# Opening chunks of two tiles by four heads, one token-major load, and later stages in an encoder trunk

## The chip, the cores and the metric

The kernel runs on one core of a Trainium2 chip. The metric is the device time of one execution in microseconds (us). Three runs of the kernel before gave 2071.57, 2072.32 and 2072.38 us, median 2072.32. Beside them one execution was recorded by the hardware profiler.

The core has TensorE (PE in the profile; its weight loads are PEld), VectorE (DVE), ScalarE (ACT), GpSimd (POOL) and SyncE (SP), which here only issues DMAs. Each takes its instructions in a fixed order and waits on semaphores.

## The reference

A trunk of two layers on 256 tokens of width 2048, all in float32. Layer 0 mixes tokens by grouped-query attention (16 query heads, 4 key and value heads of width 128, RMS norm on queries and keys, axial rotary positions), layer 1 by a gated linear recurrence in two directions. A SwiGLU feed-forward of inner width 5632 follows each.

```python
def attention_mixer(h, w_qkv, q_gain, k_gain, w_o, cos, sin):
    qkv = h @ w_qkv
    q, k, v = jnp.split(qkv, [N_Q_HEADS * HEAD_DIM, (N_Q_HEADS + N_KV_HEADS) * HEAD_DIM], axis=-1)
    ...
    q = apply_axial_rope(rms_norm(q, q_gain), cos, sin) * (HEAD_DIM ** -0.5)
    k = apply_axial_rope(rms_norm(k, k_gain), cos, sin)
    ...
    return o @ w_o

def swiglu(h, w_gate, w_up, w_down):
    return (jax.nn.silu(h @ w_gate) * (h @ w_up)) @ w_down

def reference(x, ...):
    for i in range(DEPTH):
        h = rms_norm(x, norm_mix[i])
        ...
        x = x + mix
        x = x + swiglu(rms_norm(x, norm_ffn[i]), ffn_w_gate[i], ffn_w_up[i], ffn_w_down[i])
    return x
```

## The kernel before, in words

The activations lie transposed: 16 tiles x_sb[k] of 128 features by 256 tokens. Every large product runs over k tiles of 128 features. To keep float32 accuracy on a faster number format, each weight and each activation is split into a high part (rounded) and a low part (the rest): ScalarE casts the raw weights to the high part (line 93), VectorE subtracts it for the low part (line 94). For one k tile TensorE multiplies the high part of the weights with both parts of the activation (512 columns) and the low part with the high part of the activation (256 columns), both into one PSUM accumulator "acc" (line 165). Such a pair is called a block here. step() counts blocks, and later(delay, fn) puts small pieces of TensorE work behind a fixed number of them, one at a time; TensorE's order is thus written out by hand. The order on the other engines and on the DMA queue of SP is made by a scheduler when the kernel is built.

Weights come in chunks of eight tiles of 128 by 128 (512 KB), in the order of the list "order". half() takes the next one: load_half loads it into a "raw" tile, casts and subtracts. raw, hi and lo have five buffers each, so chunks are cast up to five ahead of TensorE.

The stages of layer 0, as far as the change touches them:

- Opening. All four key heads are accumulated at once in the four accumulators. A key chunk holds four k tiles of two heads. The first chunk is loaded and split in three pieces (2, 2 and 4 tiles) with x in between; load_x loads x tiles and scales them by the norm's gain at once (ScalarE line 252, VectorE line 255, tile "xg"). Ten idle matmuls (line 229) stand ahead of it.
- The norm's mean square per token is folded in later: token_squares loads x token-major in four chunks, each into a raw tile, in between the last key and the first value chunks, and squares it on ScalarE (line 335). first_rms, FIRST = 17 blocks after the keys, makes the sums and spreads them by a small matmul (line 359).
- Keys. key(h) evacuates the accumulator (ScalarE copy line 208, VectorE add line 209), rotates, squares (line 381); KEYS blocks later a matmul sums the squares (line 388), and the key is scaled and split into kT[h]. Values are transposed 21 blocks after their product and split into vt[h].
- Queries. attend(h): evacuation, rotation on POOL (on VectorE for the last head), split into qs (lines 213, 214). Then, after delays that USUAL or LATE give: sums (transposes and squares), scores (six matmuls, the maxima on VectorE at lines 447 and 448, Exp on ScalarE, POOL scales the probabilities at line 457), turn (four transposes, copies to pT), values (six matmuls). The delays of turn and values count from the stage before.
- Output. output() runs the first half of k for four columns (FRONT), then k tiles 8 to 13 of two more chunks that it holds, then flush() runs all stages that still wait, and only then do k tiles 14 and 15 follow. The same function ends the recurrence of layer 1, whose last act tiles are made at line 651 and split at lines 213 and 214. Afterwards the norm's sums are spread by a matmul (line 274), NORM = 9 blocks later.
- Feed-forward. Units (gate and up columns) in three parts of 16, 14 and 14, each followed by its down product over 16 columns. Between parts one unit of the next part is computed ahead of the down product; the last part has none.

## Time and profile before

| what | value |
|---|---|
| median of three runs | 2072.32 us |
| the profiled execution's own time | 2072.61 us |
| its span on the core | 2070.8 us |
| granted TensorE clock, mean over the span | 0.999 |
| ScalarE, share of the span busy | 52% |
| POOL, share of the span busy | 19% |
| DMA, mean over the span | 187 GB/s |
| read from HBM | 382.13 MB |

The rows quoted further on come from the page of this execution and from answers of its trace. A row of a timeline starts with the start and the length in us, then engine, line, operation, out<-in, shape and count; in brackets stands the idle time of the engine just before it and what ended it. A row of waits reads: who waited for whom, us in total, times, longest. A row that groups instructions gives busy us and the mean ns of one, then the idle time before them. A row of windows gives the stretch, its length, then busy us and count of PE, PEld, DVE, ACT and POOL (or of PE alone), the granted TensorE clock, the busy share of the DMA engines and GB/s. Line numbers are those of the kernel before.

### The profile page before, as it was taken

The numbers are of one execution on the slowest core, as the hardware profiler recorded it, in microseconds if no ns is written. First come the engines' busy times: TensorE is split into PE (matmuls) and PEld (weight loads), VectorE is DVE, ScalarE is ACT, GpSimd is POOL, SyncE is SP. The second block draws the span as 40 slices with busy tenths as digits, with TensorE's granted clock in tenths as the row PEclk, the third lists the DMA queues.
The fourth block names the chain that finished last, engine by engine and source line by source line (L and its number), as shares of the span: only waits on it lengthen the run. The fifth ranks groups of instructions, "written<-read, shape, count | busy, mean of one in ns | idle before, by whom it ended". The sixth has DMA issues, their size and how long they took to land.

```text
span 2070.8 us, 32880 instructions
## 1 busy us (share of the span) xinstructions
PE 2060.8 (100%) x12528; PEld 1829.3 (88%) x12528; DVE 1448.1 (70%) x2152; ACT 1069.3 (52%) x1603; POOL 389.0 (19%) x394
## 2 busy tenths in 40 slices
PE   9999999999999999999999999999999999999999
PEld 7898888888888888888999998888888888888888
DVE  7889876665666666668878878766665666666665
ACT  7666444443344434444589995544443444444442
POOL 1463521110011000113334433311100111001100
PEclk9999999999999999999999999999999999999999
DMA  8544655555555565556655545555555555565564
GB/s 296 166 138 148 218 184 186 191 191 186 192 186 191 176 192 201 184 183 187 195 178 178 190 153 193 182 191 190 192 186 190 188 189 184 183 202 186 192 191 136
DMA packets 112766, 386.39 MB, mean 187 GB/s; under 512 B 12640, under 2 KB 15072, under 8 KB 112608
## 3 DMA queue, kind: packets, MB, share of 16 engines
q1 hardware_dynamic: 112464, 384.26, 56.5%
q8 instruction: 99, 1.62, 0.3%
q14 instruction: 59, 0.48, 0.1%
q10 hardware_dynamic: 144, 0.02, 0.0%
HBM read 382.13 MB, written 2.10 MB: 186 GB/s over the span
## 4 chain that ended last, share of the span: by engine, by line
PE 91%; POOL 4%; DVE 3%; issue 1%; ACT 1%; DMA 0%; SPq 0%; POOLq 0%; ACTq 0%; DVEq 0%
PE acc L165 80%; PE acc L175 3%; PE acc L176 3%; PE acc L177 3%; POOL hb L374 2%; DVE lo L94 1%; PE pm L176 1%; PE pm L177 1%; PE pm L175 1%; POOL pr L457 1%; POOL hq L375 1%; POOL hq L376 1%; ACT L309 0%; DMA raw<-in_w_k_dram 0%; ACT sg L309 0%
## 5 line engine op out<-in xcount | busy, mean ns | idle before, releaser
L94 DVE TENSOR_TENSOR lo<-raw,hi 128x1024 fp32r<-128x1024 f32 (+1 forms) x722 | 886.4, 1228 | 352.9 <-ACT hi L93 343.5
L93 ACT CAST hi<-raw 128x1024 fp32r<-128x1024 f32 (+1 forms) x722 | 741.7, 1028 | 594.6 <-PE acc L165 409.7
L165 PE MATMUL acc<-xg,hi 128*128 128x512 f32 x3200 | 1013.3, 396 | 1.8 <-DVE xg L255 1.7
L165 PEld LDWEIGHTS acc<-xg,lo 128*128 128x128 f32 x3200 | 601.4, 188 | 142.0 <-DVE lo L94 3.1
L165 PE MATMUL acc<-xg,lo 128*128 128x256 f32 x3200 | 638.4, 279 | 1.0 <-DVE lo L94 0.9
L165 PE MATMUL acc<-act,hi 128*128 128x512 f32 x1892 | 596.5, 396 | 0.1
L165 PEld LDWEIGHTS acc<-xg,hi 128*128 128x128 f32 x3200 | 490.7, 189 | 2.9 <-DVE xg L255 2.2
L165 PEld LDWEIGHTS acc<-act,lo 128*128 128x128 f32 x1892 | 355.4, 188 | 84.8 <-DVE act L213 1.3
L165 PE MATMUL acc<-act,lo 128*128 128x256 f32 x1892 | 372.9, 278 | 1.0 <-DVE act L213 1.0
L525 POOL TENSOR_TENSOR fg<-fg,nr 128x256 f32<-128x256 f32 x88 | 118.7, 1349 | 1187.3 <-ACT fg L309 1187.3
L165 PEld LDWEIGHTS acc<-act,hi 128*128 128x128 f32 x1892 | 288.9, 189 | 0.3 <-DVE act L214 0.3
L175 PE MATMUL acc<-xg,hi 128*128 128x256 f32 x512 | 144.8, 283 | 0.0
L176 PE MATMUL acc<-xg,hi 128*128 128x256 f32 x512 | 144.6, 282 | 0.0
L177 PE MATMUL acc<-xg,lo 128*128 128x256 f32 x512 | 144.4, 282 | 0.0
L208 ACT COPY fg<-acc 128x256 f32<-128x256 f32 x88 | 33.0, 375 | 152.9 <-PE acc L165 152.9
L208 ACT COPY fu<-acc 128x256 f32<-128x256 f32 x88 | 32.9, 374 | 148.2 <-PE acc L165 148.2
L177 PEld LDWEIGHTS acc<-xg,lo 128*128 128x128 f32 x512 | 97.9, 191 | 0.0
L175 PEld LDWEIGHTS acc<-xg,hi 128*128 128x128 f32 x512 | 97.9, 191 | 0.0
L176 PEld LDWEIGHTS acc<-xg,hi 128*128 128x128 f32 x512 | 97.9, 191 | 0.0
L209 DVE TENSOR_TENSOR fg<-acc,fg 128x256 f32<-128x256 f32 x88 | 37.4, 425 | 79.7 <-ACT fg L208 79.6
L209 DVE TENSOR_TENSOR fu<-acc,fu 128x256 f32<-128x256 f32 x88 | 37.4, 425 | 74.3 <-ACT fu L208 74.3
L291 DVE TENSOR_TENSOR x<-x,acc 128x256 f32<-128x256 f32 x126 | 52.9, 420 | 41.8 <-PE acc L165 41.8
(171 smaller groups left out, 1435.5 us busy)
## 6 DMA issues: line engine op xcount, KB each, us to landing
raw<-in_w_gate_dram SPq DMA_DIRECT2D x176, 512.0 KB, 3.6
raw<-in_w_up_dram SPq DMA_DIRECT2D x176, 512.0 KB, 3.6
raw<-in_w_down_dram SPq DMA_DIRECT2D x128, 512.0 KB, 3.6
raw<-in_w_in_dram SPq DMA_DIRECT2D x64, 512.0 KB, 3.9
raw<-in_w_down_dram SPq DMA_DIRECT2D x64, 384.0 KB, 3.1
raw<-in_w_qv_dram SPq DMA_DIRECT2D x40, 512.0 KB, 3.8
raw<-in_w_o_dram SPq DMA_DIRECT2D x32, 512.0 KB, 3.7
raw<-in_w_out_dram SPq DMA_DIRECT2D x32, 512.0 KB, 3.7
```

Of the source, the lines that this page charges most:

```text
L93: act.copy(hi[:, sl, :], raw[:, sl, :])
L94: dve.tensor_tensor(lo[:, sl, :], raw[:, sl, :], hi[:, sl, :].bitcast(F32), ALU.subtract)
L165: pe.matmul(o, w, x, start=(k == 0 and not part), stop=(k == total - 1 and not part))
L175: pe.matmul(o, hi, x[:, :S], start=start, stop=False)
L176: pe.matmul(o, hi, x[:, S:], start=False, stop=False)
L177: pe.matmul(o, lo, x[:, :S], start=False, stop=stop)
L208: act.copy(t, acc[:, S:])
L209: dve.tensor_tensor(t, acc[:, :S], t, ALU.add)
L291: dve.tensor_tensor(x_sb[j], x_sb[j], acc[:, :S], ALU.add)
L374: eng.tensor_tensor(b[64 * j : 64 * j + 64], y[64 * i : 64 * i + 64], s[64 * i : 64 * i + 64], ALU.mult)
L375: eng.tensor_tensor(dst, y, c, ALU.mult)
L525: pool.tensor_tensor(g, g, norm.r, ALU.mult)
```

## The change

- The key chunks are cut otherwise: the first six hold two k tiles of all four heads, the last two four k tiles of two heads (KEY_TILES). The first chunk is loaded whole and split in four pieces, the second in two. x tiles are loaded as before, but scaled in pairs, one pair ahead of each chunk's cast, and held in ScalarE's order behind the newest cast (follow).
- The token-major x becomes one 2 MB load into a tile of its own (x_tok), placed on SP behind the first two value chunks, which are taken ahead of the keys' evacuation. When its squares are done, the same place ("kv") holds kT and vt. Its squares run in two pairs, one after the evacuation of keys 0 and 1, one after the cast of the fourth value chunk.
- FIRST goes from 17 to 22, KEYS to (29, 31, 35, 41); the first head has its own delays (FIRST_HEAD), and the last three heads have new ones (LATE).
- The split of a query into qs is issued 8 blocks after its product (OPERAND) and held on VectorE behind the newest maxima, those of the head before.
- output() holds three chunks instead of two (HELD), so 18 blocks instead of 12 stand ahead of flush(); the norm behind it is finished 11 blocks later instead of 9.
- In the last part of a feed-forward, the first two columns of the down product are begun together: first half of k for both, then second half of both.

```diff
 FRONT = 4
+HELD = 3
-FIRST = 17
+FIRST = 22
 NORM = 9
-KEYS = (24, 26, 30, 33)
+KEYS = (29, 31, 35, 41)
 VALUE = 21
+FIRST_HEAD = (17, 22, 16, 10)
 USUAL = (17, 22, 15, 7)
-LATE = ((10, 23, 15, 13), (5, 15, 17, 9))
+LATE = ((17, 22, 15, 12), (10, 23, 15, 13), (7, 16, 16, 9))
+OPERAND = 8
...
+KEY_TILES = [[(2 * i + k, j) for j in range(NKV) for k in range(2)] for i in range(KT // 2 - 2)]
+KEY_TILES += [[(KT - 4 + k, j + h) for h in range(2) for k in range(4)] for j in (0, 2)]
...
+    def follow(i, j):
+        tc.add_manual_dep(i.ins, j.ins.name, ...)
+        return i
...
-    def load_half(src, n, pieces=None):
+    def load_half(src, n, pieces=1, then=None):
...
+        newest["load"] = sync.dma_start(out=raw[:, :n, :], in_=src[:, :n, :])
+        if then:
+            then()
+        for i in range(pieces):
+            sl = slice(i * n // pieces, (i + 1) * n // pieces)
+            newest["cast"] = act.copy(hi[:, sl, :], raw[:, sl, :])
             dve.tensor_tensor(lo[:, sl, :], raw[:, sl, :], hi[:, sl, :].bitcast(F32), ALU.subtract)
...
-            seq += more[:1] + [halves(w[f"w_down{l}_{p}"][j], n) for j in range(KT)] + more[1:]
+            down = [halves(w[f"w_down{l}_{p}"][j], n) for j in range(KT)]
+            if not more:
+                down[:2] = [down[j][i : i + 1] for i in range(2) for j in range(2)]
+            seq += more[:1] + down + more[1:]
...
         if n == 0:
-            x2 = [partial(load_x, 2 * i, 2) for i in range(2)]
-            return load_half(*order[n], ((0, 2, x2[0]), (2, 4, x2[1]), (4, HALF, None)))
-        if n < KT // 2 and n % 2 == 0:
-            load_x(2 * n, 4)
+            load_x(0, 2)
+            scale_x(0)
+            return load_half(*order[n], 4, partial(load_x, 2, 2))
+        if n == 1:
+            scale_x(1)
+            return load_half(*order[n], 2)
+        if n < KT // 2:
+            if n % 2 == 0:
+                load_x(2 * n, 4)
+            if n < KT // 2 - 1:
+                scale_x(n)
         if n == KT // 2 - 2:
+            scale_x(n + 1)
             load_tables()
-        if KT // 2 - 1 <= n < KT // 2 + 3:
-            token_squares(n - KT // 2 + 1)
+        if n == KT // 2 + 2:
+            tiles = load_half(*order[n])
+            token_squares(1)
+            return tiles
...
-        late = [half() for j in range(2)]
+        late = [half() for j in range(HELD)]
...
-            if j < 2:
+            if j < HELD:
...
-        norm.finish_later()
+        norm.finish_later(NORM + 2)
...
+    def scale_x(i):
+        for k in range(2 * i, 2 * i + 2):
+            j = n0.scale(k)
+            if i:
+                follow(j, newest["cast"])
...
-    def token_squares(c):
-        raw = wp.tile([P, HALF, P], F32, tag="raw", name=nm("raw"), bufs=5)
-        sync.dma_start(out=raw, in_=w["xt"][c])
-        act.activation(raw, raw, AF.Square, accum_out=msq[:, c // 2, c % 2 : c % 2 + 1])
+    x_tok = ap.tile([P, 2, D], F32, tag="kv", name="x_tok", bufs=1)
+    def token_squares(a):
+        for i in range(2):
+            t = x_tok[:, a, i * D // 2 : (i + 1) * D // 2]
+            newest["cast"] = follow(act.activation(t, t, AF.Square, accum_out=msq[:, a, i : i + 1]), newest["cast"])
...
-    for i in range(2 * KT // 4):
+    for chunk in KEY_TILES:
         wt = half()
-        for j in range(2):
-            blocks(k_acc[2 * (i % 2) + j], wt[4 * j : 4 * j + 4], n0.xs, 4 * (i // 2))
+        for i in range(0, HALF, 2):
+            blocks(k_acc[chunk[i][1]], wt[i : i + 2], n0.xs, chunk[i][0])
...
+    first_value = [half() for _ in range(2)]
+    follow(sync.dma_start(out=x_tok, in_=w["xt"]), newest["load"])
     for h in range(NKV):
+        if h == 2:
+            token_squares(0)
         key(h, k_acc[h])
...
-        split(qs, q)
+        def operand():
+            i = split(qs, q)
+            if "mx" in newest:
+                follow(i, newest["mx"])
...
-            dve.tensor_tensor(mx, mx, f, ALU.mult)
+            newest["mx"] = dve.tensor_tensor(mx, mx, f, ALU.mult)
...
+        later(OPERAND, operand)
...
+            begun = []
+            if last:
+                begun = [new_acc() for _ in range(2)]
+                for k0 in (0, HALF):
+                    for acc in begun:
+                        blocks(acc, half(), cur, k0, n)
...
-                    add_residual(j, project(cur), nxt if last else None)
+                    add_residual(j, begun.pop(0) if begun else project(cur), nxt if last else None)
```

More of the change, by code (lines that the diff above doesn't have):

```diff
@@ L87, in load_half @@
         lo = wp.tile([P, HALF, P], F32R, tag="lo", name=nm("lo"), bufs=5)
-        for a, b, then in pieces or ((0, n, None),):
-            sl = slice(a, b)
-            sync.dma_start(out=raw[:, sl, :], in_=src[:, sl, :])
-            if then:
-                then()
-            act.copy(hi[:, sl, :], raw[:, sl, :])
+        newest["load"] = sync.dma_start(out=raw[:, :n, :], in_=src[:, :n, :])
[4 more added lines that the diff above has]
+            newest["cast"] = act.copy(hi[:, sl, :], raw[:, sl, :])
             dve.tensor_tensor(lo[:, sl, :], raw[:, sl, :], hi[:, sl, :].bitcast(F32), ALU.subtract)
@@ L166, in blocks, with project @@
                 step()
-    def project(xs):
+    def project(xs, ready=()):
         acc = new_acc()
         for k0 in range(0, len(xs), HALF):
-            blocks(acc, half(), xs, k0, len(xs))
+            blocks(acc, ready.pop(0) if ready else half(), xs, k0, len(xs))
         return acc
@@ L203, in output, with evac @@
             add_residual(j, acc, norm)
-        norm.finish_later()
-    def evac(acc, tag):
+        norm.finish_later(NORM + 2)
+    def evac(acc, tag, after=None):
         t = tmp(tag, bufs=3 if tag == "hy" else 2)
-        act.copy(t, acc[:, S:])
+        i = act.copy(t, acc[:, S:])
+        if after is not None:
+            newest["cast"] = follow(i, after)
         dve.tensor_tensor(t, acc[:, :S], t, ALU.add)
@@ L265, in square, with finish_later @@
                 pool.tensor_tensor(self.ss, self.ss, sq, ALU.add)
-        def finish_later(self):
-            later(NORM, self.finish)
+        def finish_later(self, delay=NORM):
+            later(delay, self.finish)
         def finish(self):
@@ L300, in table_op @@
         if prev[0] is not None:
[L301 to L305 removed]
+            follow(i, prev[0])
         prev[0] = i
@@ L378, in key @@
     def key(h, acc):
-        y = evac(acc, "hy")
-        sq = tmp("hsq")
+        y = evac(acc, "hy", newest["cast"])
+        sq = tmp("hsq" if h < 2 else "hq")
         act.activation(sq, y, AF.Square)
@@ L416, in trunk @@
     for h in range(NKV):
-        value(h, project(n0.xs))
+        value(h, project(n0.xs, first_value))
     sync.dma_start(out=pk[:, PK0:], in_=w["pk"][:, PK0:])
```

41 lines of the change are left out of this document (23 added, 18 removed).

## The prediction

> **What bounds the kernel now.** I read the page first, its engines and then, with the view of waits, who makes TensorE wait.
>
> ```profile
> span 2070.8 us, 32880 instructions
> ...
> PE 2060.8 (100%) x12528; PEld 1829.3 (88%) x12528; DVE 1448.1 (70%) x2152; ACT 1069.3 (52%) x1603; POOL 389.0 (19%) x394
> ```
>
> ```profile
> PE acc L165 <- DVE xg L255: 1.7, 2, 1.4
> ...
> PE acc L165 <- DVE act L213: 1.0, 1, 1.0
> PE acc L165 <- DVE lo L94: 0.9, 1, 0.9
> PE pm L176 <- DVE pT L467: 0.7, 1, 0.7
> PE pm L388 <- ACT hsq L381: 0.6, 1, 0.6
> PE pm L274 <- POOL ss L265: 0.4, 2, 0.2
> ```
>
> TensorE is busy for all but 10.0 us of the span, and the diff adds and removes no matmul. So only gaps can move, and they are single gaps in single places. Their real cost is more than these rows say, because a matmul that waits for its weights or follows a gap is drawn longer. I therefore price each gap by the distance between the starts of neighbouring matmuls, in the timeline, less the usual distance:
>
> ```profile
> 5.39 0.50 PE L165 MATMUL acc<-xg,hi 128*128 128x512 f32 x1 [0.26 <-DVE xg L255]
> ...
> 31.11 0.63 PE L165 MATMUL acc<-xg,hi 128*128 128x512 f32 x2
> ...
> 31.81 0.63 PE L165 MATMUL acc<-xg,hi 128*128 128x512 f32 x2
> 33.38 0.51 PE L165 MATMUL acc<-xg,lo 128*128 128x256 f32 x2 [0.94 <-DVE lo L94]
> ```
>
> From 31.11 to 31.81 lie two k tiles (four matmuls), so one "block" (hi and lo of one k tile) costs 0.348 us, a 256-column matmul a third of that, 0.12, a 512-column one 0.23, and a chunk of eight blocks 2.79. The pair at 31.81 is the last of the keys and, 0.23 later, the first of the values: the key stage ends at 32.04. It began at 5.39 and has 64 blocks, 22.3 us; it took 26.65, so 4.3 us are lost inside it and 5.4 ahead of it.
>
> **Part 1, the opening.** Before, the first matmul needs 128 KB of weights and 256 KB of x; after, x of two tiles and one whole chunk, 768 KB, but that chunk then feeds eight blocks (four heads) instead of two. A landing of the same 768 KB is in the trace, x tiles 2 and 3:
>
> ```profile
> 6.68 0.91 ACT L252 ACTIVATE xg<-x,pk 128x256 fp32r<-128x256 f32 x2 [1.16 <-DMA x<-in_x_dram]
> ...
> 11.48 1.71 ACT L252 ACTIVATE xg<-x,pk 128x256 fp32r<-128x256 f32 x4 [0.43 <-DMA x<-in_x_dram]
> ```
>
> ```profile
> 7.70:12.30 4.60, 4.45 (x13) 2.86 (x13) 2.31 (x5) 2.48 (x5) 0.00 (x0) 0.63 1.01 370
> ```
>
> ```profile
> 10.00:15.00 5.00, 4.96 (x24) 0.87 1.02 410
> ```
>
> ```profile
> L94 DVE TENSOR_TENSOR lo<-raw,hi 128x1024 fp32r<-128x1024 f32 x19 | 24.1, 1271 | 3.1 <-ACT hi L93 3.1
> ...
> L93 ACT CAST hi<-raw 128x1024 fp32r<-128x1024 f32 x20 | 20.7, 1048 | 1.4 <-PE acc L165 0.7 <-DMA raw<-in_w_k_dram 0.6
> ...
> L208 ACT COPY hy<-acc 128x256 f32<-128x256 f32 x8 | 2.9, 368 | 3.3 <-PE acc L165 3.3
> ...
> L93 ACT CAST hi<-raw 128x256 fp32r<-128x256 f32 x2 | 0.8, 399 | 1.1 <-DMA raw<-in_w_k_dram 1.1
> ```
>
> The quarter cast (0.40) makes the first real matmul start near 7.1, 1.7 later than now. What ends last is the third chunk. Through it both orders carry the same bytes (three chunks, eight x tiles). The 512 KB ahead of it land at 11.48, 512 KB more at 410 GB/s need 1.28, so it lands at 12.8; the two scalings (0.43 each from the x4 row) fit ahead of it; cast to 13.8, low part to 15.0. The 16 blocks ahead need 5.6 us from 7.1, plus 1.7 if 3.4 us of it run at half clock (the 0.63 over 4.6 us is just that: 2 x 0.37 x 4.6 = 3.4): 14.4, inside the 15.0. So the keys end at 15.0 + 6 x 2.79 - 0.23 = 31.5, against 32.04: gain 0.5. Per chunk ScalarE needs 1.05 + 0.86 and VectorE 1.27 + 0.84 (its x share, as ScalarE's), under 2.79; the four table scalings (1.8 us) come once. Ends: the third chunk 0.6 us earlier and PE bound, gain 1.1; a second slow clock stretch, loss 1.2 (rival below).
>
> Here a rule stands against the change. The trace shows the granted clock at half after the gap around 7 us, and the change widens the gap from the warm-up's end to the first real matmul. The Trainium skill, "TensorE: Matmul & The Clock Gate", Part 1, says that TensorE's clock halves after an idle window of about 3.4 us and that the window runs free of the kernel's start; the trace agrees in the length of the slow stretch. By that page the phase could differ from run to run, and the sum would be worse by up to 1.7 us.
>
> **Part 2, values and token squares.** The low part of the first value chunk came late: 33.38 - 32.04 - 0.23 = 1.1, and 0.1 of drawn-out matmuls: 1.2. After, the first two value chunks are loaded and cast ahead of the keys' evacuation, and the four token loads that held weight buffers among them become one 2 MB load behind them, into the place where keys and values will lie later. On SP everything from the third value chunk stands behind it. Does it come in time?
>
> ```profile
> 22.94 1.06 ACT L335 ACTIVATE raw<-raw 128x1024 f32<-128x1024 f32 x1
> ...
> 24.11 1.05 ACT L93 CAST hi<-raw 128x1024 fp32r<-128x1024 f32 x1
> ...
> 35.61 0.69 DVE L349 TENSOR_TENSOR ms<-msq 128x2 f32<-128x2 f32 x1
> ...
> 37.30 0.70 DVE L354 TENSOR_SCALAR ms<-ms 128x2 f32<-128x2 f32 x1
> ```
>
> The last key chunk, cast at 24.11, ends 7.1 MB of traffic; after needs 2.56 MB more up to the end of the token load: 6.4 us at 400 GB/s, landing 30.5. ScalarE's queue behind it: two squares (22.94 to 24.11, 1.17 each) to 32.8, evacuations of keys 2 and 3 (0.37 each) to 33.6, cast of the third value chunk to 34.6, two squares to 37.0, cast of the fourth to 38.0. On VectorE the short sums (35.61 to 38.00 now: 2.4) then run from 37.0 to 39.4 and the fourth chunk's low part to 40.6. TensorE wants it at 31.5 + 24 x 0.348 + 0.23 + 0.6 (the rms matmuls) = 40.7. It just fits, so I book 0.2 of new stall; a landing a microsecond late costs 0.9, and if the token load took the place of the old stall in full, 1.2.
>
> **Part 3, held stages.** The rows of the other gaps:
>
> ```profile
> 47.45 0.70 PE L388 MATMUL pm<-hsq,ones 128*128 128x256 f32 x2 [0.56 <-ACT hsq L381]
> ...
> 79.27 0.28 PE L165 MATMUL acc<-xg,lo 128*128 128x256 f32 x1
> ...
> 80.55 0.36 PE L165 MATMUL acc<-xg,lo 128*128 128x256 f32 x1
> ...
> 103.12 0.28 PE L165 MATMUL acc<-xg,lo 128*128 128x256 f32 x1
> ...
> 103.59 0.36 PE L165 MATMUL acc<-xg,lo 128*128 128x256 f32 x1
> ...
> 104.02 0.28 PE L175 MATMUL pm<-kT,qs 128*128 128x256 f32 x1
> ```
>
> ```profile
> 178.03 0.39 PE L165 MATMUL acc<-act,hi 128*128 128x512 f32 x1
> ...
> 183.97 0.35 PE L175 MATMUL pm<-pT,vt 128*128 128x256 f32 x1
> 185.06 0.39 PE L176 MATMUL pm<-pT,vt 128*128 128x256 f32 x1 [0.74 <-DVE pT L467]
> ```
>
> ```profile
> 276.45 0.28 PE L165 MATMUL acc<-xg,lo 128*128 128x256 f32 x1
> 276.93 0.71 PE L274 MATMUL pm<-ss,ones 128*128 128x128 f32 x4 [0.21 <-POOL ss L265]
> ```
>
> ```profile
> 1255.54 0.28 PE L165 MATMUL acc<-act,lo 128*128 128x256 f32 x1
> ...
> 1257.24 0.73 PE L165 MATMUL acc<-act,hi 128*128 128x512 f32 x2
> ```
>
> Keys: the sums of squares (47.45; 0.56 idle, with the drawn-out matmuls about 0.9, as 0.74 idle below is 1.0) move from 30 to 35 blocks behind the keys while their squares stand directly behind the fourth value cast, at 38; gain 0.9 (0.6 at least).
>
> First head: across its four transposes 80.55 - 79.27 = 1.28, where a later head has 103.59 - 103.12 = 0.47: a cost of 0.8, and the transposes' wait is for the probabilities from POOL. They go one block and one set of scores (six matmuls of 0.12) later, 1.1 us, and its maxima no longer stand behind the next head's split, which waits for POOL. But the second half of its transposed scores now stands behind that split and a low part (1.27); ten blocks to its use cover about that. Gain 0.5, from 0 to 0.8.
>
> Last heads: 185.06 - 183.97 - 0.12 = 1.0. Head 13's values move from 7 to 12 blocks behind its transposes, 1.7 us, which covers it. In exchange the last head's split gets the maxima and a low part ahead of its second half. It now ends at
>
> ```profile
> 184.25 0.42 DVE L214 TENSOR_TENSOR qs<-hq,qs 128x256 fp32r<-128x256 f32 x1
> ```
>
> 184.67, 6.6 after the queries end (178.03); 1.2 more is 7.8. The last scores want it after 16 blocks (5.6), four transposes (0.35), a set of scores (0.7), two transposes (0.2) and two matmuls of their own (0.25), 7.1: stall 0.7 at worst, 0.3 taken, since the low part may be done first. Gain 0.7, from 0.3 to 1.0.
>
> Norm sums of both output stages: 276.93 - 276.45 - 0.12 = 0.36 and 0.1 behind it; two blocks later (0.7) cover it; twice, gain 0.9. What hides the later reciprocal root is the first unit: its gate is complete only 5 blocks later, and two buffers follow.
>
> Recurrence end: from 1255.54 to 1257.24 lie two steps of 0.12; it took 1.70, so 1.46, and 0.1 of drawn-out matmuls behind it, on the act tile's split (L213). HELD = 3 puts six more blocks (2.1) ahead of the flush; the last tile ends near 1257.2, TensorE comes at 1255.66 + 2.09 = 1257.75. Gain 1.5. Three of five weight buffers are then held, but they go free at 0.7, 1.4 and 2.1 us, and the next missing chunk is wanted 7.7 us after the flush against 2.3 for cast and low part.
>
> Down begun in twos: no gap of its stage is among the waits, and the same matmuls run: 0. Were that cover gone, a block or two.
>
> In a steady head the split of the next query comes to stand behind the maxima; before, it stands ahead of them:
>
> ```profile
> 99.73 0.29 DVE L213 CAST qs<-hq 128x256 fp32r<-128x256 f32 x1 [0.50 <-POOL hq L376]
> ...
> 100.40 0.16 DVE L448 TENSOR_TENSOR mx<-mx,hf 128x2 f32<-128x2 f32 x1
> ```
>
> VectorE idled 0.50 for POOL ahead of the split, so the maxima (0.16) fit in there and the new order costs nothing; no head between the first and the last ones waits now, so it gains nothing either.
>
> **The sum.** 0.5 + 1.2 - 0.2 + 0.9 + 0.5 + 0.7 + 0.9 + 1.5 = 6.0 us. The profiled execution's span of 2070.8 (time 2072.6) becomes 2064.8 (2066.6); against the median of 2072.3, 2066.3. I say 2066.4.
>
> **Rivals.** (a) The stalls move: fourth value chunk, first and last head give back what they gained (1.0 + 0.5 + 0.7), 2068.6. For: all three stand within 0.5 us of their limits. Against: the limits are met on paper.
> (b) The opening starts cold: the clock gate grants half speed for a second stretch of 3.4 us, TensorE bound, 1.7 more: 2068.1. The trace has one slow stretch only. By the Trainium skill's page named above, it would hang on the phase.
> (c) Slower: the split held behind the maxima. VectorE's queue would stop in each of 15 heads until the maxima are done, scores would wait, and nothing fills TensorE. The split's halves end by 100.5, ahead of the maxima at 100.40 to 100.56, and the scores that read it start at 104.02: it decides from 3.5 us of delay on. At 4.2 it is 15 x 0.7 = 10.5 us: 2076.9. Against: the maxima no longer wait for POOL.
> (d) The change doesn't do what it says: VectorE's and ScalarE's queues are as full as before, and each gap closed opens again a little later; 2072. Against: in the first 60 us the casts wait for TensorE to free a buffer (0.7 in the cast's row) more than for loads (0.6), so there is lead to give.
>
> **How the numbers follow.** Forecast 62%, (a) 13%, (b) 9%, (c) 8%, (d) 8%. A change of 0.2%, 4.1 us, is what a measurement can tell. Faster takes the forecast, (b) and a third of (a): 0.75; within it the rest of (a) and (d): 0.17; slower (c): 0.08. All gaps closed and the opening at its best end gives 6.0 + 0.6 + 0.2 + 0.3 + 0.3 = 7.4 and, with half a microsecond between runs, 2064.4; upward 2070.2 takes in (a) and (b) and leaves out (c) and (d).
>
> **What would show it.** First real matmul near 7.1; keys ended near 31.5; no wait of L165 for a low part near 32; the token squares starting near 30.5; no wait at the two norm sums nor at the first act tile after the recurrence; small waits at most at the first head's values and the last head's scores. Wrong if heads in the middle take longer than now, if the granted clock shows more than one slow stretch, or if ScalarE stands idle before the squares while TensorE waits.

## The result and the profile after

The changed kernel takes 2065.64 us (median of seven runs, 2065.10 to 2066.09) against 2072.33 us of the kernel before (median of seven runs). The ratio is 0.9966, 95% interval 0.9957 to 0.9975. That is 6.7 us less, where 5.9 were forecast (2066.4). The profiled execution took 2065.64 us, its span is 2063.9 us against 2070.8.

From here on the line numbers in a row are those of the kernel that it comes from. In the changed kernel 197 is the matmul of a block (165 before), 112 and 113 are cast and low part (93, 94), 287 and 290 scale x (252, 255), 207 to 209 are the small matmuls of scores and values (175 to 177), 516 is a head's transposes (463), 519 and 520 copy what they give out of PSUM as high and low part (ScalarE, VectorE), 508 and 510 are the reciprocal and POOL's scaling of the probabilities (455, 457), 248 is the second half of a query's split (214).

The page of the changed kernel, span and engines, and then all that the view of waits has for TensorE (who waited for whom, us in total, times, longest):

```profile
span 2063.9 us, 32882 instructions
...
PE 2057.1 (100%) x12528; PEld 1828.5 (89%) x12528; DVE 1451.2 (70%) x2154; ACT 1069.4 (52%) x1605; POOL 390.9 (19%) x394
```

```profile
PE pm L264 <- POOL ones L261: 1.0, 1, 1.0
PE acc L197 <- ACT hi L112: 0.9, 1, 0.9
PE pm L208 <- DVE pT L520: 0.7, 1, 0.7
PE acc L197 <- DVE lo L113: 0.4, 1, 0.4
PE pm L516 <- POOL pr L510: 0.4, 1, 0.4
PE pm L209 <- DVE qs L248: 0.2, 1, 0.2
```

The waits at the first act tile after the recurrence, at the keys' sums of squares and at the two norm sums are no longer in the list. What stands in it: the start (1.0), the first real matmul (0.9), one low part (0.4, the third chunk's) and three waits in the heads.

The timeline of TensorE in the changed kernel, in order of time: the opening, the end of the keys, the first head's values, the second head's transposes, the end of the queries, the last scores.

```profile
6.10 0.50 PE L197 MATMUL acc<-xg,hi 128*128 128x512 f32 x1 [0.94 <-ACT hi L112]
...
12.84 0.51 PE L197 MATMUL acc<-xg,lo 128*128 128x256 f32 x2 [0.42 <-DVE lo L113]
...
29.20 0.62 PE L197 MATMUL acc<-xg,hi 128*128 128x512 f32 x2
...
81.34 0.28 PE L207 MATMUL pm<-pT,kv 128*128 128x256 f32 x1
82.27 0.39 PE L208 MATMUL pm<-pT,kv 128*128 128x256 f32 x1 [0.66 <-DVE pT L520]
...
83.68 0.27 PE L516 MATMUL pm<-cn,pr 128*128 128x128 f32 x1
84.34 0.55 PE L516 MATMUL pm<-cn,pr 128*128 128x128 f32 x3 [0.39 <-POOL pr L510]
...
174.31 0.39 PE L197 MATMUL acc<-act,hi 128*128 128x512 f32 x1
...
181.39 0.28 PE L208 MATMUL pm<-kv,qs 128*128 128x256 f32 x1
181.82 0.38 PE L209 MATMUL pm<-kv,qs 128*128 128x256 f32 x1 [0.15 <-DVE qs L248]
```

The pair at 29.20 is the last matmul of the keys and the first of the values, so the key stage ends at 29.20 + 0.23 = 29.43; before, 32.04. The output projection begins at 174.31; before, at 178.03. So the 6.9 us of the span are made up of 2.6 in the opening, 1.1 from the values to the last query (this stretch lasted 145.99 and lasts 144.88), and 3.2 behind the queries. The forecast had 0.5, 2.4 and 3.1. That the total was right is luck in good part: two steps were wrong, in opposite directions. The opening gained 2.1 more than booked, and the first heads lost 1.0 where a gain of 0.5 was booked.

ScalarE in the opening of the changed kernel, from its timeline, and two views of windows (stretch, length, busy us and count of PE, PEld, DVE, ACT, POOL, granted clock, DMA share, GB/s), first the changed kernel, then the kernel before:

```profile
9.20 0.91 ACT L287 ACTIVATE xg<-x,pk 128x256 fp32r<-128x256 f32 x2
10.47 1.05 ACT L112 CAST hi<-raw 128x1024 fp32r<-128x1024 f32 x1 [0.36 <-DMA raw<-in_w_k_dram]
```

```profile
4.00:6.00 2.00, 1.16 (x8) 0.97 (x7) 1.03 (x3) 1.26 (x4) 0.00 (x0) 1.00 1.03 363
6.00:8.00 2.00, 1.90 (x9) 1.49 (x10) 1.92 (x6) 1.84 (x7) 0.00 (x0) 1.00 0.97 393
```

```profile
4.00:6.00 2.00, 1.74 (x12) 1.50 (x11) 1.52 (x4) 1.21 (x3) 0.00 (x0) 1.00 0.79 231
6.00:8.00 2.00, 0.60 (x4) 0.28 (x3) 0.85 (x3) 0.91 (x2) 0.00 (x0) 0.97 1.01 319
8.00:10.00 2.00, 1.91 (x5) 1.02 (x4) 0.70 (x2) 0.62 (x1) 0.00 (x0) 0.50 1.00 348
```

Two things differ that the forecast had equal. The scaling at 9.20 is that of x tiles 4 and 5; the load that carries them is the last of the first 2 MB. Before, the load that ends the same 2 MB let its scaling start at 11.48: the same bytes are there at least 2.3 us earlier (at 9.20 ScalarE did not wait for them any more), because DMA moves 363 instead of 231 GB/s from 4 to 6 us, and 393 instead of 319 from 6 to 8. The third chunk's cast starts at 10.47, where its load was predicted for 12.8. And the granted clock (the number behind POOL's) is half from 8 to 10 us before, and full through the opening after. Either could be the cause of the 2.1 us.

### The profile page after: what moved, and what is told of

It reads as the page before. It is cut to its first block, busy times and chain, and to the rows that moved or that the text cites. A ratio compares the mean times of both kernels' runs of the same rounds, so it can differ in the third digit from the quotient of the medians.

```text
span 2063.9 us, 32882 instructions
## 1 busy us (share of the span) xinstructions
PE 2057.1 (100%) x12528; PEld 1828.5 (89%) x12528; DVE 1451.2 (70%) x2154; ACT 1069.4 (52%) x1605; POOL 390.9 (19%) x394
## 4 chain that ended last, share of the span: by engine, by line
PE 96%; DVE 2%; issue 0%; DMA 0%; ACT 0%; POOL 0%; SPq 0%; DVEq 0%; POOLq 0%
PE acc L197 83%; PE acc L207 3%; PE acc L208 3%; PE acc L209 3%; PE pm L209 1%; PE pm L207 1%; PE pm L208 1%; DVE lo L113 1%; DMA raw<-in_w_k_dram 0%; PE pm L516 0%; ACT hi L112 0%; PE pm L488 0%; DVE hv L497 0%; DVE hy L243 0%; DVE hf L323 0%
```

## The experiments

Each edit is given against the kernel that is named. A microsecond is small beside the intervals of the ratios (about 0.0012 each way, 2.5 us), so a verdict below rests on the place in the profile, with the median of the runs beside it. The kernel before took 2072.23 to 2072.40 beside all of them, so their medians can be set against each other.

### The opening: loads, clock or shape

first_whole is the kernel before with one load for the first weight chunk:

```diff
+        if pieces:
+            load_x(0, 2)
+        sync.dma_start(out=raw[:, :n, :], in_=src[:, :n, :])
         for a, b, then in pieces or ((0, n, None),):
             sl = slice(a, b)
-            sync.dma_start(out=raw[:, sl, :], in_=src[:, sl, :])
...
-            return load_half(*order[n], ((0, 2, x2[0]), (2, 4, x2[1]), (4, HALF, None)))
+            return load_half(*order[n], ((0, 2, None), (2, 4, x2[1]), (4, HALF, None)))
```

> The kernel before, with only the form of its first loads changed: the first x pair is asked for ahead of the first weight chunk, and that chunk comes in one load of 512 KB (4 KB per partition) instead of three (1, 1 and 2 KB per partition). The order of the matmuls is untouched. Theory A (the opening's gain comes from loads that land earlier): the first 768 KB are there near 5.7 us instead of 6.7, the third chunk's cast starts near 11.7 instead of 12.7, the keys end about 1 us earlier, time 2071.3. Theory B (it comes from the new shape of the chunks, which feed TensorE longer): the first real matmul only starts later (about 6.1 instead of 5.4), the third chunk's cast stays near 12.7, and the keys end at 32.0 or later, time 2072.3 to 2073.

bridge is the kernel before with more idle matmuls in the hole of the opening:

```diff
                 step()
+            if clock[0] == 2:
+                warm = ps_m.tile([P, P], F32, tag="pm", name=nm("pm"))
+                for _ in range(7):
+                    pe.matmul(warm, ones, ones, start=True, stop=True)
```

> The kernel before, with seven more warm-up matmuls (into a PSUM tile that nobody reads) placed behind the first four real ones, where TensorE stood idle for 1.6 us. Nothing else is changed. Theory C (the clock): the half-clock stretch from 7.9 to 11.3 goes away and the keys end up to 1.7 us earlier, time 2070.6. Theory A (the loads bind): the stretch goes away, but the third chunk lands when it did (cast near 12.7), so TensorE only waits there, the gain is 0 to 0.4 us, time 2072.0 to 2072.3.

cold is the changed kernel with `WARM = 4` instead of 10.

> The changed kernel with 4 instead of 10 warm-up matmuls at its start; nothing else is changed. Theory C (the clock): the granted clock is half for at least one stretch of 3.4 us from about 4.5 on; of the matmuls from 6.1 on some 1.8 us worth run at half speed, and as the third chunk leaves 0.7 us of slack the keys end 1.0 to 1.7 us later, time 2066.7 to 2067.4. If the clock does not matter here (loads bind): 2065.6 to 2066.0.

old_opening is the changed kernel with the opening of before (key chunks, loads and scalings as in the lines that the change's diff removes):

```diff
-KEY_TILES = [[(2 * i + k, j) for j in range(NKV) for k in range(2)] for i in range(KT // 2 - 2)]
-KEY_TILES += [[(KT - 4 + k, j + h) for h in range(2) for k in range(4)] for j in (0, 2)]
+KEY_TILES = [[(4 * (i // 2) + k, 2 * (i % 2) + j) for j in range(2) for k in range(4)] for i in range(KT // 2)]
```

> The changed kernel with the opening of the kernel before (chunks of four tiles by two heads, first chunk in three loads, x scaled where it is loaded); everything behind the keys as changed. If the opening is worth what the trace suggests, the keys end near 32.0 instead of 29.3 and the time is 2065.6 + 2.7 = 2068.3. If it is worth the 0.5 us that was forecast and the rest of the gain sits elsewhere: 2066.1. If the earlier end of the keys also let the later stages in the attention go wrong (first heads), less than 2.7: about 2067.4.

pieces is the changed kernel with four loads for the first chunk:

```diff
-        newest["load"] = sync.dma_start(out=raw[:, :n, :], in_=src[:, :n, :])
+        loads = pieces if then else 1
+        for i in range(loads):
+            sl = slice(i * n // loads, (i + 1) * n // loads)
+            newest["load"] = sync.dma_start(out=raw[:, sl, :], in_=src[:, sl, :])
```

> The changed kernel with its first weight chunk asked for in four loads of 128 KB (1 KB per partition) instead of one of 512 KB; order of loads, casts and matmuls as changed. Theory A1 (small pieces slow the first loads): the second x pair lands at 7.5 or later instead of 6.3, the third chunk at 11.7 or later instead of 10.45, the keys end 1 us or more later, time 2066.6 or more. Theory A2 (what helped is that x is asked for first, the size of the pieces does not matter): landings as in the changed kernel, the first real matmul up to 0.8 us earlier (5.3), but the third chunk's low part binds as it did, keys' end and time the same: 2065.5.

Measured:

| kernel | median, us | ratio to before, 95% | scaling of x tiles 4, 5 starts | keys end |
|---|---|---|---|---|
| before | 2072.33 | | 11.48 | 32.04 |
| first_whole | 2070.08 (11 runs) | 0.9990, 0.9981 to 0.9998 | 9.42 | 29.97 |
| bridge | 2072.33 (11 runs) | 0.9996, 0.9988 to 1.0005 | 10.82 | 31.38 |
| changed | 2065.64 (7 runs) | 0.9966, 0.9957 to 0.9975 | 9.20 | 29.43 |
| cold | 2066.34 (5 runs) | 0.9966, 0.9953 to 0.9978 | 9.42 | 30.73 |
| old_opening | 2067.60 (8 runs) | 0.9975, 0.9965 to 0.9986 | 11.56 | 32.19 |
| pieces | 2066.99 (8 runs) | 0.9975, 0.9964 to 0.9985 | 10.79 | 31.03 |

The loads first. ScalarE's timeline of first_whole, TensorE's in it, and one of its windows:

```profile
9.42 1.71 ACT L254 ACTIVATE xg<-x,pk 128x256 fp32r<-128x256 f32 x4 [0.22 <-DMA x<-in_x_dram]
```

```profile
29.74 0.63 PE L167 MATMUL acc<-xg,hi 128*128 128x512 f32 x2
...
34.25 0.51 PE L167 MATMUL acc<-xg,lo 128*128 128x256 f32 x2 [1.09 <-DVE lo L96]
```

```profile
4.00:6.00 2.00, 1.02 (x8) 0.82 (x7) 1.04 (x4) 1.35 (x4) 0.00 (x0) 1.00 1.02 385
```

The same window of pieces, its ScalarE and its end of the keys:

```profile
4.00:6.00 2.00, 2.00 (x11) 1.78 (x11) 1.61 (x6) 1.77 (x5) 0.00 (x0) 1.00 0.84 206
```

```profile
10.79 0.91 ACT L290 ACTIVATE xg<-x,pk 128x256 fp32r<-128x256 f32 x2
```

```profile
30.80 0.63 PE L200 MATMUL acc<-xg,hi 128*128 128x512 f32 x2
```

The rate from 4 to 6 us goes with the form of the first loads and with nothing else that was varied: 231 and 206 GB/s with the first chunk in pieces (before and pieces, x asked for second and first), 385 and 363 with the chunk whole (first_whole and changed); the other runs fall in with this (last section). With the keys' ends this makes a table of two by two: four tiles by two heads, 32.04 in pieces and 29.97 whole; two tiles by four heads, 31.03 and 29.43. The form of the load is worth 2.1 and 1.6 us, the new shape 1.0 and 0.5. The medians say the same of the form: 2.3 (2070.08, with 2072.40 for the kernel before beside it) and 1.35 (2066.99 against 2065.64). The 2.1 has the clock in it, which is half for 3.4 us in the kernel before and full in first_whole; in the 1.6 neither kernel has such a stretch. Theory A, and A1 of its two forms, hold, though the keys' end moved twice as far as theory A had it (1 us); A2 falls. In pieces the first real matmul did come 0.8 us earlier (5.28), as A2 had it, and TensorE then waited 1.6 for the second chunk.

SP's timelines show a part of how this comes about. There a request stands for 0.4 to 0.5 us, so with the first chunk in four requests the load of x tiles 4 to 7 is issued at 4.01 (pieces) instead of 2.60 (changed), 1.4 later, and their scaling starts 1.6 later. In three requests it is issued at 3.54 (before) instead of 2.59 (first_whole), 0.95 later, and the scaling starts 2.1 later. So the number of requests may be most of the one difference and half of the other; no run parts it from their size.

In first_whole the gain was passed on. Its values' stage lost about 1.1 of it again: the row at 34.25 shows a low part that is 1.25 late (1.1 before), a second one is 0.5 late at 37.62, and the matmuls that spread the first norm's sums are 0.7 late. But the keys' sums of squares (0.9 before) and half of the first head's wait were then in time, and the output projection begins 2.5 earlier (175.54 against 178.03).

The clock. In bridge the stretch at half clock is gone (its pairs of 512-column matmuls take 0.63 from 9.03 on, where one takes 1.51 at 8.70 before), the keys end 0.66 earlier, and the time is that of the kernel before. Its loads happened to be 0.66 earlier as well (10.82 against 11.48), and TensorE waited for the third chunk (0.58 idle at 11.81). So the half clock cost the kernel before nothing that these runs can tell: the loads bound, and theory C falls as the cause of the gain. In cold the loads come early and the half clock shows its price: the keys end 1.3 later, as theory C had it, but the time is below what it expected (2066.34 against 2066.7 at the least). The span is only 0.6 longer (2064.5 against 2063.9), because the low part that was late at 38 us and the query split that was late at 69 us are then in time. old_opening shows the same cover: its keys end 2.76 later than those of the changed kernel, its time is 2.0 more, which is the third of the expected outcomes (2067.4; measured 2067.60). From the keys' end to the output projection both take 0.6 less than the changed kernel (144.23 and 144.25 against 144.88): so much of a later opening is covered.

### The first heads: late copies or held splits

first_usual is the changed kernel with `FIRST_HEAD = (17, 22, 15, 7)`, the usual delays.

> The changed kernel with the usual distances (17, 22, 15, 7) for the first head instead of (17, 22, 16, 10), so that its four transposes come ahead of the second head's scores again. Theory D (the later transposes put ScalarE's two copies behind the second head's reciprocal root, and that is what delays them): the copies come at 76 instead of 77.9 us, the 0.8 at the first head's values and the 0.55 at the second head's transposes go away; the transposes' own wait for POOL (0.4 to 0.8, as before) comes back; time 0.7 us less: 2064.9. Theory E (the splits held behind the maxima make VectorE late there, whatever the transposes' place): the second half of the transposed scores stays behind the maxima and the split, its use now comes 1.4 us earlier, so the stall at the values grows to 1.5 and more, time 2066.5 to 2067.

split_at_once is the changed kernel without the hold:

```diff
-        def operand():
-            i = split(qs, q)
-            if "mx" in newest:
-                follow(i, newest["mx"])
+        split(qs, q)
...
-        later(OPERAND, operand)
```

> The changed kernel with each query's split issued where it was before, without the hold of 8 blocks and without the order behind the maxima. Theory E (the hold makes VectorE late in the first heads): the stalls there (0.8 + 0.1 + 0.55, and 0.3 at the first scores) go, as does the 0.3 at the last scores, time 2064.0 to 2064.4. Theory D (the transposes' place does it): they stay as they are, time 2065.5 to 2066. In the steady heads both expect no wait, 7.65 us a head as now; if the hold is needed there, each of some 12 heads loses a few tenths, 2067 to 2069.

values_later is the changed kernel with `FIRST_HEAD = (17, 22, 16, 13)`.

> The changed kernel with the first head's values 13 instead of 10 blocks behind its transposes; nothing else is changed. Theory D (ScalarE's copies come 1.4 us late behind the second head's root; the values only lack the time): three blocks are 1.05 us, the stall of 0.8 + 0.1 at the values goes away, the 0.55 at the second head's transposes stays, because VectorE's reciprocal still stands behind the late second half: time 2064.8. Theory F (the wait is a ring, so that whatever is issued later waits later): the values wait as long as now, 2065.6.

Medians: first_usual 2064.91 us (ratio 0.9964, 0.9950 to 0.9978), split_at_once 2064.98 (0.9965, 0.9953 to 0.9978), values_later 2065.28 (0.9966, 0.9953 to 0.9978).

To read them, VectorE's, ScalarE's and POOL's timelines of the changed kernel behind the first head's transposes (issued at 76.47):

```profile
77.58 0.20 ACT L341 ACTIVATE rsq_s<-hv 128x2 f32<-128x2 f32 x1 [1.37 <-DVE hv L497]
...
77.92 0.35 ACT L519 CAST pT<-pm 128x256 fp32r<-128x256 f32 x1
...
79.53 0.37 ACT L519 CAST pT<-pm 128x256 fp32r<-128x256 f32 x1 [0.30 <-DVE pT L520]
```

```profile
80.67 1.22 DVE L113 TENSOR_TENSOR lo<-raw,hi 128x1024 fp32r<-128x1024 f32 x1
81.80 0.42 DVE L520 TENSOR_TENSOR pT<-pm,pT 128x256 fp32r<-128x256 f32 x1
82.14 0.16 DVE L508 RECIPROCAL rs<-sm 128x2 f32<-128x2 f32 x1
```

```profile
82.39 1.90 POOL L510 TENSOR_SCALAR pr<-pr,rs 128x256 f32<-128x256 f32 x2 [2.43 <-DVE rs L508]
```

This is one chain. The later transposes stand behind the second head's scores, so on ScalarE the copies (L519) stand behind the second head's root (L341), which waits 1.37 us for VectorE. The second copy ends at 79.9; by then VectorE has taken up the next split and a low part of 1.22, and its half of the transposed scores (L520) comes at 81.80. TensorE waits for it at 82.27. Behind it stands the second head's reciprocal at 82.14, behind that POOL's scaling at 82.39, and for that TensorE waits at 84.34: the two stalls have one cause.

first_usual, TensorE and ScalarE:

```profile
76.00 1.00 PE L516 MATMUL pm<-cn,pr 128*128 128x128 f32 x4 [0.27 <-POOL pr L510]
```

```profile
77.03 0.38 ACT L519 CAST pT<-pm 128x256 fp32r<-128x256 f32 x1 [0.29 <-PE pm L516]
```

The first copy stands ahead of the root again, at 77.03 instead of 77.92, both stalls are gone, and the transposes wait for POOL as they did before (from 75.45 to 76.00, and drawn out by 0.34: 0.77 in all, less than the 1.48 of the two stalls). Theory D's time was 2064.9, the median is 2064.91; that they meet so closely is chance, as the five runs lie between 2064.36 and 2065.45. The profiled execution is the slowest of them. Its keys end at 29.78, 0.35 later than those of the changed kernel, and a low part of the values (39.14) and the first scores (69.55) wait 0.3 more in all, so its span is only 0.2 below. What shows the 0.7 is the place, 0.77 against 1.48.

split_at_once keeps both stalls (0.82 + 0.1 and 0.63): theory E falls. Yet it is 0.66 faster than the changed kernel, for another reason: the two small waits for the split itself are gone, at the first scores (0.28 with its drawn-out neighbour) and at the last ones (0.41). The view of the tile qs tells what the hold did; first the changed kernel, then split_at_once (what VectorE idled for ahead of the split, us in total and times):

```profile
  DVE qs L248: 0.7, 3
  POOL hq L415: 0.4, 1
```

```profile
  POOL hq L415: 6.3, 12
```

Without the hold VectorE idles 6.3 us for POOL over 12 heads, and no steady head is slower for it. The hold took away idle time that cost nothing. (Both kernels end their keys alike, at 29.41 and 29.43, so here the spans may be compared as well: 2063.1 and 2063.9.)

In values_later the stall moved instead of going; TensorE's timeline:

```profile
81.89 0.38 PE L208 MATMUL pm<-pT,kv 128*128 128x256 f32 x1
...
82.57 0.30 PE L516 MATMUL pm<-cn,pr 128*128 128x128 f32 x1
83.96 0.55 PE L516 MATMUL pm<-cn,pr 128*128 128x128 f32 x3 [1.09 <-POOL pr L510]
```

The values wait 0.14 instead of 0.82, and the second head's transposes 1.28 instead of 0.55. Neither expectation was right: the sum (1.4) is what the chain above leaves, and more distance at its first use only hands it to the second.

### The later stages, undone together

late_undone is the changed kernel with four edits taken back:

```diff
-HELD = 3
+HELD = 2
...
-LATE = ((17, 22, 15, 12), (10, 23, 15, 13), (7, 16, 16, 9))
+LATE = (USUAL, (10, 23, 15, 13), (5, 15, 17, 9))
...
-            if not more:
-                down[:2] = [down[j][i : i + 1] for i in range(2) for j in range(2)]
...
-        norm.finish_later(NORM + 2)
+        norm.finish_later()
...
-            if last:
+            if False:
                 begun = [new_acc() for _ in range(2)]
```

> The changed kernel with four later edits undone at once, each of which can be read at its own place: two chunks held instead of three, norm sums after 9 instead of 11 blocks, the last down projection not begun in twos, and the last heads' distances as before. If the stages are worth what the two traces suggest: 1.5 us of stall at the first act tile after the recurrence, 0.46 at each of the two norm sums, about 1.0 at head 13's values in place of the 0.4 at the last scores, nothing at the down projections: span 2063.9 + 1.5 + 0.9 + 0.6 = 2066.9, time 2068.7. If beginning down in twos covers something that the trace does not show as a wait: up to 0.7 more for each of two layers, 2069.4 to 2070.

Median 2069.18 us (11 runs; ratio 0.9985, 0.9977 to 0.9994), span 2067.3. TensorE's timeline at the three places:

```profile
179.83 0.28 PE L205 MATMUL pm<-pT,kv 128*128 128x256 f32 x1
181.81 0.39 PE L206 MATMUL pm<-pT,kv 128*128 128x256 f32 x1 [1.70 <-DVE pT L518]
...
273.20 0.28 PE L195 MATMUL acc<-xg,lo 128*128 128x256 f32 x1
273.68 0.71 PE L308 MATMUL pm<-ss,ones 128*128 128x128 f32 x4 [0.20 <-POOL ss L299]
...
1252.29 0.28 PE L195 MATMUL acc<-act,lo 128*128 128x256 f32 x1
1253.25 0.39 PE L195 MATMUL acc<-act,lo 128*128 128x256 f32 x1 [0.69 <-DVE act L245]
1253.71 0.73 PE L195 MATMUL acc<-act,hi 128*128 128x512 f32 x2
```

Less the usual 0.12 each, the recurrence's end costs 0.84 + 0.34 and 0.1 behind it, 1.3, a norm sum 0.36 and 0.1 behind it (two of them, 0.9), head 13's values 1.86 and 0.1 behind it. The last is twice what it cost before the change with the same distances for the last heads; what of the other edits doubled it was not tried apart. It is also why the time lies between the two expected outcomes (2068.7, and 2069.4 to 2070): head 13's values had been put at 1.0. Set against the 0.4 at the last scores that it replaces, the four edits are worth 1.3 + 0.9 + 1.5 = 3.7 us by their places. The spans differ by 3.4, but late_undone reached the output projection 0.4 earlier (at 173.90, against 174.31), so behind that it took 3.8 more. No more than 0.1 is left over for the down products begun in twos. The four edits were not undone one by one; what each is worth is read from its place.

### A kernel that beats both

heads_mended is the changed kernel with the splits at once, the usual delays for the first head, and

```diff
-                eng.tensor_scalar(pr[:, a, :], pr[:, a, :], rs[:, a : a + 1], 1.0, ALU.mult, ALU.mult)
+                (eng if h else dve).tensor_scalar(pr[:, a, :], pr[:, a, :], rs[:, a : a + 1], 1.0, ALU.mult, ALU.mult)
```

> The changed kernel with three edits at the heads: each query's split issued at once, the usual distances for the first head, and the first head's probabilities scaled on VectorE instead of POOL. Theory D: with the copies ahead of the second head's root the two stalls (0.93 and 0.55) go; the transposes' wait for POOL (0.77 in the run with the usual distances alone) goes too, as VectorE scales the probabilities in about 0.6 directly behind its reciprocal; the small waits at the first and the last scores (0.28 and 0.41) stay away as in the run with the splits at once. Sum 2.2 us: time 2063.4 to 2063.8. If VectorE's two extra scalings push the next low part into TensorE's way, a stall of some 0.5 at the projection beside it: 2064.1.

all_mended has one more edit:

```diff
-        return load_half(*order[n])
+        return load_half(*order[n], 2 if n == 2 else 1)
```

> The kernel of the run heads_mended with one more edit: the third weight chunk is cast in two halves, so that its first low part comes about 1.1 us earlier. If the third chunk's low part alone binds the opening: the 0.58 + 0.11 at 12.8 us goes, keys' end 0.6 earlier, time 2062.8 to 2063.2, the fastest of all. If the next chunk or the values' low part is then late by as much: no gain over heads_mended.

heads_mended: 2064.15 us (five runs, 2063.89 to 2064.71; ratio 0.9960, 0.9948 to 0.9973). Its profile has no wait of 0.15 or more left in TensorE between 66 and 85 us but one at the first head's transposes:

```profile
75.18 0.28 PE L197 MATMUL acc<-xg,lo 128*128 128x256 f32 x1
75.55 0.81 PE L512 MATMUL pm<-cn,pr 128*128 128x128 f32 x4
```

They cost 0.25, and 0.15 in their own spacing, instead of 0.77, since VectorE scales the probabilities in 0.62. The time is 0.35 above the expected range's upper end. It is that of the second outcome (2064.1), but the stall that this put at a low part is not there. The profiled execution, the slowest of the five, had slow loads and ended its keys at 30.10 (see the last section); whether that holds for the others their times alone do not tell. all_mended: 2064.30 us (five runs, 2063.78 to 2064.71; ratio 0.9960, 0.9946 to 0.9973). The third chunk's stall is gone and the keys end at 28.81, the earliest of all runs, but the two places that a late opening had covered opened: 0.45 at a low part of the values (38.33) and 0.27 at the first scores. No gain over heads_mended can be told, which was the second of the expected outcomes. Every run of either is faster than every run of the changed kernel (2065.10 at the least), with 2072.23 for the kernel before beside them; values_later, which keeps both stalls' cost, took 2065.22 to 2066.02 in the same round. The intervals of the ratios overlap with that of the changed kernel, so that either is faster rests on these runs and on the places.

## Why the prediction was right, and which of its steps were not

- **The opening, booked 0.5, gave 2.6** at the keys' end, and 2.0 in the time (old_opening). The step that failed is that "both orders carry the same bytes", with the landing taken from the trace of before (11.48). The bytes are the same, but the time that they need is not a property of the bytes: with the first chunk whole the 2 MB were there by 9.2 to 9.4. first_whole alone, on the kernel before, moved the keys' end by 2.07. The Trainium skill says both things of it, in "Perfetto Trace Analysis", DMA Optimizations: larger transfers use the memory better, and splitting may let some work start sooner. The runs show both (the first real matmul 0.8 earlier in pieces) and which of them decided here: the keys' end was 1.6 later.
- **The third chunk as the bound of the opening** was right as a place: TensorE waits for its low part at 12.84, predicted at 15.0. The first real matmul came at 6.10, predicted near 7.1, for the same reason as above.
- **Rival (b), a second half-clock stretch,** did not come; there was none at all. Of the experiments only old_opening has a stretch at half clock after the clock had once been full (0.75 of the clock from 8 to 12 us and 0.82 from 12 to 16, that is 3.4 us at half). first_whole has none, though TensorE idles as long there (0.75 ahead of the matmul at 7.96, 0.78 ahead of that at 7.85 in old_opening), nor has pieces, where it idles 1.58 ahead of the matmul at 10.19. So the length of one gap does not decide. The Trainium skill, "TensorE: Matmul & The Clock Gate", Part 1, lets this hang on the phase of a window that runs free; no run here tests that. The two slow stretches followed gaps of 1.40 (before) and 0.78, well under the idle window of about 3.4 us that the prediction names; what sets them off stays open. The price of 1.7 was too high: bridge shows none in the kernel before, where the loads hide it, and cold shows 1.3 at the keys' end and 0.6 in the span of the changed kernel.
- **Values and token squares, booked 1.2 less 0.2,** gave about 0.9 (read from the waits; no run undoes this part alone). The second pair of squares stands behind the cast of the third value chunk, as the working has it, and not of the fourth, as the list of changes says. The result: the old stall is gone, and the fourth value chunk's low part is 0.3 late at 37.8 to 38.9. The squares were forecast to start at 30.5 and start at 29.38; but TensorE came 2.1 earlier than forecast, so a limit that was just met on paper was just missed.
- **Keys' sums, booked 0.9,** 0.9: the wait is gone. This too is read from the waits alone.
- **The first head, booked +0.5, gave -1.0** (0.28 + 0.93 + 0.55 after, 0.8 before). The step that failed is "ten blocks to its use cover about that". It counted what stands ahead of the second half on VectorE, and not that ScalarE's copies, moved behind the second head's scores, fall behind that head's root. first_usual shows it: moving them back takes 0.7 off. The sign "small waits at most at the first head's values" did not come true.
- **Last heads, booked 0.7,** about 0.6: head 13's stall of 1.0 + 0.1 is gone, the last scores wait 0.31 + 0.1 for the split's second half, where 0.3 was taken.
- **Norm sums 0.9, recurrence end 1.5, down 0.** The first two are gone from the waits after; undone, they come back with 0.9 and 1.3. The down products show nothing in either direction.
- **Steady heads 0, rival (c).** Right: the hold costs the steady heads nothing. split_at_once adds that it saves them nothing either.

With the measured terms the sum is 2.6 + 0.9 + 0.9 - 1.0 + 0.6 + 0.9 + 1.5 = 6.4; the spans differ by 6.9, and the remaining 0.5 lies in gaps too small to be named one by one. Rival (a), stalls that move, was half true: the first heads gave back more than they had to gain, and the opening, whose best end was put 0.6 above its booking, paid for it. That the total came out within 0.8 us is luck: two errors of opposite sign.

## What to carry to other kernels

A landing time read from a trace belongs to the requests that stood ahead of it, their number and sizes included; when a change alters the form of the first loads, take the rate from a stretch with loads of the new form. When a stage is moved on TensorE, look at what the engines behind it (here ScalarE's copies) will then stand behind, and follow the chain to its second use, because distance given to the first use alone hands the stall on. Idle time that an instruction causes on an engine off the path, like the 6.3 us of VectorE ahead of the splits, is no reason to move it.

## What the runs showed of the hardware

The rate of the loads from 4 to 6 us goes with the form of the first 512 KB of weights: 206 to 231 GB/s in the four kernels that load them in pieces of 1 or 2 KB per partition (pieces, old_opening, bridge, before), 328 to 385 in the nine that load them with 4 KB. From 12 to 20 us all thirteen move 406 to 414. Whether it is the size of the pieces or their number that slows them was not tried apart.

The opening varies from one execution to the next with the same loads. values_later and heads_mended differ in nothing before 60 us; TensorE's row that ends the keys, in the one and in the other:

```profile
28.75 0.63 PE L197 MATMUL acc<-xg,hi 128*128 128x512 f32 x2
```

```profile
29.87 0.63 PE L197 MATMUL acc<-xg,hi 128*128 128x512 f32 x2
```

1.1 us lie between them. The table of two by two, with one execution for each of its four ends, stands above this for the form of the loads (1.6 and 2.1), and the medians bear it out; it does not for the shape of the chunks (0.5 and 1.0).

The granted clock in the view of windows reads 1.00 until its first record, whatever the clock is: in cold the windows from 4 to 10 us have 1.00, while the matmuls there run at half speed until about 10.8. TensorE's timeline of cold:

```profile
9.82 1.05 PE L197 MATMUL acc<-xg,hi 128*128 128x512 f32 x2
...
10.99 0.63 PE L197 MATMUL acc<-xg,hi 128*128 128x512 f32 x2
```

A pair of 512-column matmuls is drawn 1.05 us long at half clock and 0.63 at full; the clock of a short stretch at the start is read from such rows.
